# The mLSTM heads of a decoder layer: from the planner's order to a written-out order on all engines

## The chip, the cores and the metric

The kernel runs on one core of a Trainium2 chip. The metric is the device time in microseconds (us). A core has five engines that work side by side: TensorE (PE) multiplies matrices into PSUM banks, VectorE (DVE) and ScalarE (ACT) do elementwise work, GpSimd (POOL) does elementwise work on SBUF, and SyncE (SP) issues most of the loads. Each engine takes its instructions in the order in which they stand in its own program, and waits on semaphores for the results of the others. ACT also issues loads, from its own queue.

## The reference, cut to what matters

One layer: a mixer with four mLSTM heads of 256 columns and a convolution group of 1024 channels beside them, then a gated feed-forward part, for 512 positions of 1024 columns in float32.

```python
mod = cond @ ada_w[l] + ada_b[l]
sh1, sc1, g1, sh2, sc2, g2 = jnp.split(mod[:, None, :], N_MOD, axis=-1)
u = rms_norm(x, mix_pre_g[l]) * (1.0 + sc1) + sh1
proj = u @ w_in[l]
qk_raw, v, o_pre, gates, glu = jnp.split(proj, [...], axis=-1)
qk = jax.nn.silu(causal_dwconv(qk_raw, qk_conv_w[l], qk_conv_b[l]))      # 4 taps
h = mlstm_chunkwise(heads(q), heads(k), heads(v), gates[..., :H] + ..., gates[..., H:] + ...)
h = rms_norm(h, ml_norm_g[l].reshape(H, Dh)).reshape(Bsz, S, D_ML)
h = (h * jax.nn.sigmoid(o_pre))
a, gt = jnp.split(glu, 2, axis=-1)
y = causal_dwconv(a * jax.nn.sigmoid(gt), cv_dw_w[l], cv_dw_b[l])        # 31 taps
y = jax.nn.silu(layer_norm(y, cv_ln_g[l], cv_ln_b[l]))
mix = jnp.concatenate([h, y], axis=-1) @ w_out[l]
x = x + g1 * rms_norm(mix, mix_post_g[l])
...
```

## The kernel before

Every product is made of three matmuls over numbers split into a high and a low part (`mm3`, L198): a weight tile of 512 columns is loaded raw, ACT copies it to the high part and POOL subtracts to get the low one (`w_split`, L176). The pool of split tiles holds 20 (`WSLOTS`), that is ten high-low pairs; raw loads have two buffers (`RAWS`).

The stages, in order: the input's norm and the first six blocks of the GLU projection (written in order), the rest of the GLU projection, the values of head 0 with the gates (`make_v(0)`, L443), the projections of head 0, then a loop over heads that attends with head h while it projects head h+1, then head 3's attention beside the first half of the output projection (`mix_first`, L694), the second half (`mixb`), and the feed-forward part.

The instructions of PE and SP keep the order of the text. Those of DVE, ACT and POOL are placed by a planner, which simulates the program and takes what is ready, by priority; `in_order()` (L74) is a context that ties the DVE, ACT and POOL instructions traced inside it to the order of the text, each engine for itself. Before the change only the opening and a later stretch are so tied.

What a head consists of:

* `head_load(h)` (L485) loads three raw matrices and splits them into twelve pieces of 512 columns.
* `head_proj(h, i)` (L491), i = 0 to 5, is one item: 24 matmuls of 512 columns. Items 0 and 1 are q, 2 and 3 are k: ACT scales (L475), DVE adds three taps (`conv4`, L477), ACT applies Silu (L478). Items 4 and 5 are the output gate: one Tanh on ACT (L503), result `so`.
* `make_E(h)` (L592): PE spreads the running maximum over the partitions (`Mb`), DVE adds the mask (`Md`, L596), ACT takes seven exponentials (L601, L603).
* `make_v(h)`: four value tiles of 24 matmuls of 256 columns, each copied out by ACT (L467).
* `attention(h)` (L508), a generator that gives way between its steps: four score blocks `s` (L516) with a DVE product each (`E`, L517); four output tiles `o` (L527) that ACT reads (L530 to L532); a factor per position (L537 to L540, `fac`), with which DVE scales `hn` four times (L543); then twice: four transposes `hT` (L549), DVE's `so` (L551), ACT's high part `hh` (L554), DVE's low part `hl` (L555).

The scores, outputs, `Mb` and `hT` share two PSUM banks (`atbank`), the projections share four (`mmbank`), the convolution and its norm two (`cvbank`).

Beside this runs the 31-tap convolution: for each of eight channel blocks DVE does 25 taps (L722, 200 in all), ACT and POOL the other five (L716, L718, `SIDE`), then a running mean and square (L732 to L737). All of it is traced once, in front of the head loop, with a low priority (`LATER`), so the planner fills DVE's free time with it. `norm_mean`, `norm_sums` and `norm_rows` (L740 to L763) close the norm. The modulation sums `ada_block(i)` (L159) load 512 KB on ACT's queue and reduce them on DVE (L167); numbers 16 to 23 are traced behind the head loop, with the low priority too, tied behind the last tap; numbers 24 to 39 are tied behind the last `hl`, and `gains` (L843 to L845), which PE turns as `gT` (L646), follow from them.

## Time and profile before

| what | us |
|---|---|
| median of 3 runs | 800.78 (800.26 to 801.73) |
| the profiled execution | 798.5 |
| its span, first to last instruction | 796.7 |
| PE busy | 779.3 |
| DVE / ACT / POOL busy | 475.6 / 380.6 / 438.8 |
| mean granted TensorE clock | 0.995 |

A line of a group gives the line of the kernel, engine, operation, what it writes and reads, the count, then the busy time and the mean of one in ns, then the engine's idle time in front of it and who ended it. A line of the waits gives who waited for whom: total, times, longest. A line of the timeline gives start, duration, engine and instruction; in brackets stands the idle time before it and who ended it. A line of the windows gives the stretch, its length, and the busy time of PE, PEld, DVE, ACT and POOL with the number of instructions, the granted TensorE clock, the busy share of the DMA engines and GB/s.

### The profile page before, as it was taken

What the parts mean: (1) busy time and instruction counts of PE and PEld (TensorE: products, weight loads), DVE (VectorE), ACT (ScalarE), POOL (GpSimd) and SP (SyncE); (2) the same over time, 40 slices, a digit from 0 to 9 for tenths busy, and PEclk for the clock granted to TensorE, in tenths of its full rate; (3) what the DMA queues carried; (4) which work ended last, traced back from release to release, by engine and by line L of the source; (5) the groups of instructions that cost most, each with busy time, mean ns of one, the idle gap of its engine ahead of it and who ended that gap; (6) DMA issues with size and microseconds to landing.
All of it is one profiled execution on the core that took longest, in us unless ns stands there. A gap on an engine that the chain in (4) does not pass through costs nothing.

```text
span 796.7 us, 10339 instructions
## 1 busy us (share of the span) xinstructions
PE 779.3 (98%) x3778; PEld 651.8 (82%) x3778; DVE 475.6 (60%) x732; ACT 380.6 (48%) x710; POOL 438.8 (55%) x359
## 2 busy tenths in 40 slices
PE   8999999999899799999999999999999999999996
PEld 6788898788788688888879988888888888888885
DVE  6779999999997434546868784454444453000014
ACT  6684548757463555571344454444444444122112
POOL 4799759959669433342751475444444444454420
PEclk9999999999999899999999999999999999999999
DMA  8964223222026331426854652222222222222205
GB/s 331 347 237 133 80 73 140 80 94 91 28 107 209 108 133 54 159 105 211 345 186 150 211 195 105 81 82 103 105 107 106 79 107 107 107 105 100 86 0 185
DMA packets 24886, 106.96 MB, mean 134 GB/s; under 512 B 2914, under 2 KB 2946, under 8 KB 17412
## 3 DMA queue, kind: packets, MB, share of 16 engines
q1 hardware_dynamic: 16164, 82.17, 28.8%
q10 hardware_dynamic: 8672, 24.13, 8.7%
q8 instruction: 30, 0.49, 0.3%
q14 instruction: 20, 0.16, 0.1%
HBM read 102.08 MB, written 4.21 MB: 133 GB/s over the span
## 4 chain that ended last, share of the span: by engine, by line
PE 72%; DVE 14%; DMA 5%; issue 3%; POOL 2%; ACT 2%; SPq 0%; DVEq 0%; ACTq 0%; POOLq 0%
PE up L201 10%; PE up L200 10%; PE up L202 10%; DVE cv L722 7%; PE dn L200 5%; PE dn L202 5%; PE dn L201 5%; PE glu L202 2%; PE glu L200 2%; PE glu L201 2%; PE qko L200 2%; PE qko L202 2%; PE qko L201 2%; DMA wglu<-in_w_glu 2%; DMA spare<-in_adaT 2%
## 5 line engine op out<-in xcount | busy, mean ns | idle before, releaser
L722 DVE SCALAR_TENSOR_TENSOR cv<-gt,cvw,cv 128x502 f32<-128x502 f32 (+23 forms) x200 | 134.1, 727 | 1.6 <-ACT cv L710 1.3
L1062 DVE TENSOR_TENSOR fo<-dn,g2r 128x512 f32<-128x512 f32 x8 | 5.5, 685 | 103.1 <-ACT dn_0junk L1058 103.1
L718 POOL TENSOR_TENSOR cs<-cs,cs 128x510 f32<-128x510 f32 (+3 forms) x32 | 43.7, 1368 | 4.4 <-ACT cs L716 4.3
L183 POOL TENSOR_TENSOR wup_1024l<-wup,wup_1024h 128x512 fp32r<-128x512 f32 x20 | 26.9, 1345 | 30.7 <-ACT wup_1024h L182 30.6
L183 POOL TENSOR_TENSOR wup_1536l<-wup,wup_1536h 128x512 fp32r<-128x512 f32 x20 | 27.1, 1354 | 29.6 <-ACT wup_1536h L182 29.5
L183 POOL TENSOR_TENSOR wup_512l<-wup,wup_512h 128x512 fp32r<-128x512 f32 x20 | 26.8, 1340 | 23.6 <-ACT wup_512h L182 21.8
L183 POOL TENSOR_TENSOR wup_0l<-wup,wup_0h 128x512 fp32r<-128x512 f32 x20 | 27.6, 1378 | 20.8 <-ACT wup_0h L182 20.7
L167 DVE SCALAR_TENSOR_TENSOR junk<-ada,cb 128x1024 bf16<-128x1024 f32 x20 | 31.6, 1580 | 8.6 <-DMA ada<-in_adaT 8.4
L201 PE MATMUL up<-u2l,wup_0h 128*128 128x512 f32 (+1 forms) x100 | 36.5, 365 | 0.2 <-DVE u2l L891 0.2
L200 PE MATMUL up<-u2h,wup_0h 128*128 128x512 f32 (+1 forms) x100 | 36.5, 365 | 0.0
L200 PE MATMUL up<-u2h,wup_1024h 128*128 128x512 f32 (+1 forms) x100 | 36.4, 364 | 0.0
L202 PE MATMUL up<-u2h,wup_1536l 128*128 128x512 f32 (+1 forms) x100 | 36.4, 364 | 0.0
L202 PE MATMUL up<-u2h,wup_0l 128*128 128x512 f32 (+1 forms) x100 | 36.4, 364 | 0.0
L200 PE MATMUL up<-u2h,wup_512h 128*128 128x512 f32 (+1 forms) x100 | 36.4, 364 | 0.0
L201 PE MATMUL up<-u2l,wup_512h 128*128 128x512 f32 (+1 forms) x100 | 36.4, 364 | 0.0
L202 PE MATMUL up<-u2h,wup_512l 128*128 128x512 f32 (+1 forms) x100 | 36.4, 364 | 0.0
L200 PE MATMUL up<-u2h,wup_1536h 128*128 128x512 f32 (+1 forms) x100 | 36.4, 364 | 0.0
L201 PE MATMUL up<-u2l,wup_1536h 128*128 128x512 f32 (+1 forms) x100 | 36.4, 364 | 0.0
L202 PE MATMUL up<-u2h,wup_1024l 128*128 128x512 f32 (+1 forms) x100 | 36.4, 364 | 0.0
L201 PE MATMUL up<-u2l,wup_1024h 128*128 128x512 f32 (+1 forms) x100 | 36.3, 363 | 0.0
L183 POOL TENSOR_TENSOR wd_1024l<-wd,wd_1024h 128x512 fp32r<-128x512 f32 x11 | 14.3, 1296 | 29.7 <-ACT wd_1024h L182 29.7
L183 POOL TENSOR_TENSOR wd_0l<-wd,wd_0h 128x512 fp32r<-128x512 f32 x11 | 14.3, 1299 | 27.3 <-ACT wd_0h L182 27.3
(729 smaller groups left out, 2620.3 us busy)
## 6 DMA issues: line engine op xcount, KB each, us to landing
wup<-in_w_up SPq DMA_DIRECT2D x22, 1024.0 KB, 4.8
wqko<-in_w_qko SPq DMA_DIRECT2D x12, 1024.0 KB, 4.8
wd<-in_w_down SPq DMA_DIRECT2D x11, 1024.0 KB, 4.8
ada<-in_adaT ACTq DMA_DIRECT2D x20, 512.0 KB, 5.9
ada<-in_adaT SPq DMA_DIRECT2D x16, 512.0 KB, 7.2
wo<-in_w_out SPq DMA_DIRECT2D x8, 1024.0 KB, 4.8
spare<-in_adaT ACTq DMA_DIRECT2D x12, 512.0 KB, 8.4
wglu<-in_w_glu SPq DMA_DIRECT2D x5, 1024.0 KB, 7.5
```

The costliest lines, as they stand in the source:

```text
L167: t = V.scalar_tensor_tensor(out=junk, in0=r, scalar=1.0, in1=cb, op0=ALU.mult, op1=ALU.mult, accum_out=mod[:, i : i + 1])
L183: (eng or G).tensor_tensor(out=lo[:, :n], in0=src, in1=hi[:, :n].bitcast(F32), op=ALU.subtract)
L200: PE.matmul(ps, a[0], b[0], start=start, stop=False)
L201: PE.matmul(ps, a[0], b[1], start=False, stop=False)
L202: PE.matmul(ps, a[1], b[0], start=False, stop=stop)
L718: G.tensor_tensor(out=side[:, d:], in0=side[:, d:], in1=t[:, d:], op=ALU.add)
L722: last_tap = V.scalar_tensor_tensor(out=cp[:, d:], in0=cvx[j][:, : T - d], scalar=w(CK - 1 - d), in1=cp[:, d:], op0=ALU.mult, op1=ALU.add)
L1062: V.tensor_tensor(out=res[hf], in0=ps, in1=g2r[hf], op=ALU.mult)
```

## The change

Everything from head 0's first projection to the last turn of head 3 stands in one `in_order()` region, so the order of the text is the order on DVE, ACT and POOL too. The weights of all heads, of the values 1 to 3 and of the first half of the output projection are one list of pieces (`spans`); `stream_to(n)` splits them up to piece n and starts the load of the next raw matrix, and each item is followed by it, `LOOK` pieces ahead. The taps and the modulation sums 16 to 23 become a generator, `filler()`: `fill(n)` writes n taps. 92 (`AHEAD`) are traced in front of the region with the low priority, the rest beside the items, as numbers in the code say. A sum comes each eight taps from tap 128 (`ADAB`). `make_v` now gives way after each tile, `attention` once more before the factor and once before `hn`; two small products of the factor move from POOL to DVE. The Silu of q and k comes after the item's taps. The norm's mean goes through the filler; its rows are spread over the output blocks, and head 3's steps come one block earlier.

```diff
+LOOK = 6
+AHEAD = 92
+ADAB = 128
+TAPS = ((4, 4, 1, 2, 5, 6),)
...
-        for q in range(0, KT, 4):
+        for q in range(0, 0 if h else KT, 4):
             r = raws.tile([P, 2048], F32, tag="raw", name=f"wv{h}_{q}")
-            nc.sync.dma_start(r[:, : 4 * n], w_v[h - 1, q // 4] if h else w_v0[q // 4])
-            if h:
-                for i in range(2):
-                    hi, lo = w_split(r[:, i * 2 * n : (i + 1) * 2 * n], f"wv{h}_{q + i}")
-                    wv += [(hi[:, :n], lo[:, :n]), (hi[:, n:], lo[:, n:])]
-            else:
-                wv += [tuple(w[:, :n] for w in w_split(r[:, i * n : (i + 1) * n], f"wv{h}_{q + i}")) for i in range(4)]
+            nc.sync.dma_start(r[:, : 4 * n], w_v0[q // 4])
+            wv += [tuple(w[:, :n] for w in w_split(r[:, i * n : (i + 1) * n], f"wv{h}_{q + i}")) for i in range(4)]
+        if h:
+            stream_to(first_of["v", h] + 4)
+            for hi, lo in vw[h]:
+                wv += [(hi[:, :n], lo[:, :n]), (hi[:, n:], lo[:, n:])]
...
-            if tt > 1:
-                yield
+            if h:
+                stream_to(first_of["v", h] + 4 + 2 * tt)
+            yield
...
-        S.activation(t, t, AF.Silu)
...
-    def head_load(h):
-        pieces = []
+
...
+    def stream_to(n):
+
+        while streamed[0] < min(n, len(spans)):
+            i = streamed[0]
+            load_to(i + 1)
+            first = max(j for j in loaded if j <= i)
+            if i == first:
+                load_to(next((j + 1 for j in range(i + 1, len(spans)) if spans[j][0] is not None), 0))
+            _, name, a, n_, dest = spans[i]
+            dest.append(w_split(loaded[first][:, a : a + n_], f"{name}_{a}"))
+            streamed[0] += 1
...
+    def item(h, i, taps, also=lambda: None):
+
+        stream_to(first_of[h] + 2 * i + 2)
+        head_proj(h, i)
+        fill((taps + 1) // 2)
+        also()
+        n = first_of[h] + 2 * i + 2
+        stream_to(n + LOOK - 1)
+        fill(taps // 2)
+        stream_to(n + LOOK)
+        if i < 4:
+            t = heads[h][1 + i // 2][-1]
+            S.activation(t, t, AF.Silu)
...
+        yield
...
-        G.tensor_tensor(out=dm, in0=dm, in1=dm, op=ALU.mult)
-        G.tensor_tensor(out=ssq, in0=ssq, in1=dm, op=ALU.add)
+        V.tensor_tensor(out=dm, in0=dm, in1=dm, op=ALU.mult)
+        V.tensor_tensor(out=ssq, in0=ssq, in1=dm, op=ALU.add)
         G.tensor_tensor(out=fac, in0=ssq, in1=mhalf, op=ALU.pow)
+        yield
...
+    def conv_taps():
+
+        cv_first(0)
+        for j in range(KT):
+            w = lambda tap: cvw[:, tap * KT + j : tap * KT + j + 1]
+            side = None
+            cp = cps_[j]
+            for d in range(SIDE + 1, CK):
+                last_tap[0] = V.scalar_tensor_tensor(out=cp[:, d:], in0=cvx[j][:, : T - d], scalar=w(CK - 1 - d), in1=cp[:, d:], op0=ALU.mult, op1=ALU.add)
+                s = d - SIDE
+                if s % 4 == 1 and s // 4 < SIDE:
+                    e = s // 4 + 1
+                    t = cvs.tile([P, T], F32, tag="cvs", name=f"cs{j}_{e}")
+                    if e == 1:
+                        V.memset(t[:, :e], 0.0)
+                    S.activation(t[:, e:], cvx[j][:, : T - e], AF.Copy, scale=w(CK - 1 - e))
+                    if side is not None:
+                        G.tensor_tensor(out=side[:, e:], in0=side[:, e:], in1=t[:, e:], op=ALU.add)
+                    else:
+                        side = t
+                if d == CK - 4 and j + 1 < KT:
+                    cv_first(j + 1)
+                yield
...
+    def ada_load(i):
+        adat[i] = adas.tile([P, D], F32, tag="ada", name=f"ada_{i}")
+        nc.scalar.dma_start(adat[i], adaT[i // 2][:, (i % 2) * D : (i % 2 + 1) * D])
+
+    def ada_sum(i):
+        junk = small.tile([P, D], BF16, tag="junk", bufs=1, name=f"junk_{i}")
+        V.scalar_tensor_tensor(out=junk, in0=adat[i], scalar=1.0, in1=cb, op0=ALU.mult, op1=ALU.mult, accum_out=mod[:, i : i + 1])
...
+    def filler():
+        sums = None
+        ada_load(16)
+        ada_load(17)
+        for n, _ in enumerate(conv_taps()):
+            if later and n % 25 == 6:
+                sums = running(*later.pop())
+            if sums is not None:
+                next(sums, None)
+            i, turn = divmod(n - ADAB, 8)
+            if 0 <= i < 8:
+                if turn == 0:
+                    ada_sum(16 + i)
+                elif turn == 3 and i < 6:
+                    ada_load(18 + i)
+            yield
...
+    tc.cur_priority += LATER
+    fill(AHEAD)
+    tc.cur_priority -= LATER
...
+    region = in_order()
+    region.__enter__()
+    stream_to(6)
+    gates_lf()
+    for i in range(3):
+        item(0, i, TAPS[0][i])
+    gates_sum()
+    fill(2)
+    item(0, 3, TAPS[0][3])
+    gates_max()
+    item(0, 4, TAPS[0][4])
+    gates_tok()
+    item(0, 5, TAPS[0][5])
+    make_E(0)
     for h in range(H - 1):
-        head_load(h + 1)
         steps = attention(h)
         if h == 0:
-            head_proj(1, 0)
+            item(1, 0, 3)
         next(steps)
-        head_proj(h + 1, 1 if h == 0 else 0)
+        fill(2)
+        item(h + 1, 1 if h == 0 else 0, 3)
         next(steps)
+        fill(1)
         if h:
-            head_proj(h + 1, 1)
-        head_proj(h + 1, 2)
+            item(h + 1, 1, 3)
+        item(h + 1, 2, 5)
         next(steps)
-        head_proj(h + 1, 3)
+        item(h + 1, 3, 5)
         next(steps)
-        head_proj(h + 1, 4)
+        item(h + 1, 4, 7)
         next(steps)
-        head_proj(h + 1, 5)
+        item(h + 1, 5, 4, lambda: next(steps))
         make_E(h + 1)
-        if h == H - 2:
-            norm_mean()
+        next(steps)
         values = make_v(h + 1)
+        fill(2)
+        next(values)
+        fill(3)
+        next(values)
+        fill(1)
         next(values)
         for _ in steps:
             pass
-        next(values)
-        if h == H - 2:
-            norm_sums()
-
-    tc.cur_priority += LATER
-    for i in range(16, 24):
-        ada_block(i, last_tap)
-    ada_done(16, 24)
-    tc.cur_priority -= LATER
-    gain(0, 16, "mix_post_g")
-    wo = {}
+        fill(2)
+        for _ in values:
+            pass
+        fill(2)
+    while not normed:
+        fill(1)
+    norm_sums()
     steps = attention(H - 1)
+    rows = norm_rows()
     next(steps)
     mix_first(0)
+    fill(2)
     next(steps)
-    norm_rows()
+    fill(1)
     mix_first(1)
+    next(rows)
+    next(rows)
     mix_first(2)
+    next(rows)
+    next(rows)
+    ada_done(16, 24)
+    gain(0, 16, "mix_post_g")
     mix_first(3)
+    next(rows)
+    next(steps)
     mix_first(4)
+    next(rows)
+    next(rows)
     next(steps)
     mix_first(5)
+    for _ in rows:
+        pass
     next(steps)
     mix_first(6)
     next(steps)
-    for n in range(7, 10):
-        mix_first(n)
+    mix_first(7)
+    next(steps)
+    mix_first(8)
+    mix_first(9)
     for _ in steps:
         pass
+    region.__exit__(None, None, None)
+    stream_to(len(spans))
...
```

Of the parts left out, the steps of the gates become functions without a change in them, and `norm_rows` gives way after each row, with the low part of a row written one row later.

More of the change, by code (lines that the diff above doesn't have):

```diff
@@ L639, in decoder_layer, with gates_tok @@
+    def gates_tok():
+        mps = atbank("mtok")
+        mv = mps[:, : NT * H].rearrange("p (t h) -> p t h", t=NT)
+        for tt in range(NT):
+            PE.matmul(mv[:, tt, :], Mr[0][:, tt * P : (tt + 1) * P], ident[:H, :H], start=True, stop=True)
+        V.tensor_tensor(out=em, in0=Fc, in1=mv, op=ALU.add)
+        S.activation(em, em, AF.Exp, scale=-1.0)
+        V.tensor_scalar(out=em, in0=em, scalar1=EPS**0.5, scalar2=None, op0=ALU.mult)
     RD = float(D) ** 0.5
@@ new lines, in decoder_layer, with running @@
+    later = []
+    def running(j, y):
+        mean_of = ys[0] if j == 1 else ysum
+        dl = cvtile(f"ydl{j}")
+        V.scalar_tensor_tensor(out=dl, in0=mean_of, scalar=-1.0 / j, in1=y, op0=ALU.mult, op1=ALU.add)
+        yield
+        yield
+        dst = ysq if j == 1 else dl
+        S.activation(dst, dl, AF.Square, scale=(j / (j + 1.0)) ** 0.5)
+        yield
+        if j > 1:
+            G.tensor_tensor(out=ysq, in0=ysq, in1=dl, op=ALU.add)
+        G.tensor_tensor(out=ysum, in0=mean_of, in1=y, op=ALU.add)
@@ new lines, in decoder_layer @@
+    adat = {}
+    def ada_load(i):
[19 more added lines that the diff above has]
+                    ada_load(18 + i)
+            yield
+        for _ in range(3):
+            yield
+        for _ in running(*later.pop()):
+            yield
+        for _ in range(7):
+            yield
+        for _ in norm_mean():
+            yield
+        normed.append(1)
+        done.append(1)
+        while True:
+            yield
```

175 lines of the change are left out of this document (95 added, 80 removed).

## The prediction

> **What bounds the kernel now.** The page's busy line comes first, then TensorE's (PE) own waits.
>
> ```profile
> PE 779.3 (98%) x3778; PEld 651.8 (82%) x3778; DVE 475.6 (60%) x732; ACT 380.6 (48%) x710; POOL 438.8 (55%) x359
> ```
> ```profile
> PE hT L549 <- ACT E L603: 3.4, 2, 2.5
> ...
> PE hT L549 <- DVE hn L543: 1.7, 2, 0.9
> PE s L516 <- DVE so L551: 1.4, 1, 1.4
> ...
> PE gT L646 <- DVE gains L844: 0.4, 1, 0.4
> ```
>
> The matmuls set the end. The change adds and removes none that matters, so it is worth only what PE now loses by waiting in the heads. The waits are 3.4 + 1.7 + 1.4 = 6.5 us, all at one place: the hand-over from one head to the next, where the transposes hT wait for `hn` and for a PSUM bank, and the scores `s` for a bank that `so` frees. Next the windows by stage: first head's attention, second, third, and a piece of the second.
>
> ```profile
> 158.00:209.20 51.20, 48.97 (x262) 41.40 (x260) 51.20 (x80) 32.20 (x69) 37.93 (x32) 1.00 0.20 72
> 209.20:270.40 61.20, 56.96 (x285) 48.04 (x286) 50.48 (x74) 33.00 (x69) 43.73 (x30) 0.94 0.42 138
> 270.40:326.40 56.00, 56.00 (x298) 47.41 (x297) 22.11 (x36) 27.83 (x60) 22.38 (x20) 1.00 0.21 76
> ...
> 262.40:269.20 6.80, 4.29 (x20) 4.00 (x20) 3.06 (x7) 5.35 (x14) 0.90 (x1) 0.50 0.29 114
> ```
>
> After the length stand PE, weight load, DVE, ACT, POOL, then the granted clock. DVE is busy 51.20 of 51.20 us in the first stretch, with PE idle for 2.23. The third, with the taps done and DVE at 22 us, has no PE idle at all. And the second stall costs twice: the clock falls to 0.50 for 6.8 us. The timeline shows who was late.
>
> ```profile
> 202.11 6.49 DVE L722 SCALAR_TENSOR_TENSOR cv<-gt,cvw,cv 128x495 f32<-128x495 f32 x10
> 202.85 0.60 PE L549 MATMUL hT<-ident,hn 128*128 128x128 f32 x4
> 204.34 0.66 PE L549 MATMUL hT<-ident,hn 128*128 128x128 f32 x4 [0.89 <-ACT E L603]
> 208.51 0.67 DVE L551 SCALAR_TENSOR_TENSOR so<-so,hT 128x512 f32<-128x512 f32 x1
> 209.24 1.13 PE L516 MATMUL s<-q_0c,k_2c 128*128 128x512 f32 x2 [1.37 <-DVE so L551]
> ...
> 211.06 0.81 PE L516 MATMUL s<-q_0c,k_2c 128*128 128x384 f32 x2
> ...
> 259.60 0.28 PE L202 MATMUL v<-wv_5h,ul 128*128 128x256 f32 x1
> 260.69 0.30 PE L549 MATMUL hT<-ident,hn 128*128 128x128 f32 x1 [0.81 <-DVE hn L543]
> 261.87 1.00 PE L549 MATMUL hT<-ident,hn 128*128 128x128 f32 x3 [0.88 <-DVE hn L543]
> 262.54 0.68 DVE L596 TENSOR_TENSOR Md<-Mb,cmask 128x512 f32<-128x512 f32 x1
> 265.38 1.12 PE L549 MATMUL hT<-ident,hn 128*128 128x128 f32 x4 [2.51 <-ACT E L603]
> 266.14 0.56 PE L200 MATMUL v<-wv_0h,uh 128*128 128x256 f32 x1
> ```
>
> hT is ready after 202.85, but ten taps run on DVE until 208.6, and `so` behind them frees the bank late. In the second hand-over `hn` is late, and `Md` with the exps behind it (262.54 to 265.38) later still: DVE did the eight modulation sums in a bunch just before.
>
> **What can be won.** First hand-over: 0.89 + 1.37 = 2.26 us. Second: the second window is 61.20 against 56.00, and the third holds two matmul groups that the second lacks:
>
> ```profile
> 312.43 0.86 PE ytot L743 x2
> ...
> 325.67 0.79 PE ry_s L208 x8
> ```
>
> So an undisturbed head is 56.00 - 1.65 = 54.35 and the second loses 6.85; by hand, 0.81 + 0.88 + 2.51 idle plus half of the 4.29 busy us at half clock (2.15) is 6.35. Together 8.6 to 9.1; I take 9.0.
>
> **The change part by part.** *Taps dealt out.* 92 taps stay ahead of the region, 24 lie in head 0's projections, then 40 in each turn of the head loop (3+2+3+1+5+5+7+4 beside the items, 2+3+1+2+2 beside the values); the last four and the norm's mean fall in the third turn. Two turns are the heavy ones. Their DVE work, from these groups (head stage):
>
> ```profile
> L722 DVE SCALAR_TENSOR_TENSOR cv<-gt,cvw,cv 128x487 f32<-128x487 f32 (+24 forms) x122 | 82.6, 725 | 0.0
> L167 DVE SCALAR_TENSOR_TENSOR junk<-ada,cb 128x1024 bf16<-128x1024 f32 x8 | 13.0, 1630 | 3.9 <-DMA ada<-in_adaT 3.9
> L477 DVE SCALAR_TENSOR_TENSOR k_2c<-qko,vec,k_2c 128x511 f32<-128x511 f32 (+2 forms) x12 | 8.9, 743 | 3.2 <-ACT k_2c L475 3.1
> ...
> L543 DVE TENSOR_SCALAR hn<-hn,fac 128x256 f32<-128x256 f32 x12 | 8.6, 773 | 2.1 <-POOL fac L540 2.1
> L517 DVE SCALAR_TENSOR_TENSOR E<-s,E 128x512 f32<-128x512 f32 (+3 forms) x14 | 7.0, 503 | 10.9 <-PE s L516 10.9
> L732 DVE SCALAR_TENSOR_TENSOR ydl<-ysum,gt 128x512 f32<-128x512 f32 x6 | 6.7, 1109 | 2.7 <-POOL gt L726 2.7
> ```
>
> 40 taps at 6.49/10 = 0.649 are 26.0; four sums (one each 8 taps from tap 128) at 1.63 are 6.5; 12 q/k taps at the same pace 7.8; four `hn` 3.1; four `E` 2.0; 1.6 running means 1.8; Md, two `so` and two `hl` (about 0.7 each) 3.5. Sum 50.7 us; the small operations on 4 or 8 columns add perhaps 1 (estimate: as one running mean). With taps at their record, 0.725, and q/k taps at 0.743, it is 50.7 + 3.0 + 1.1 + 1 = 55.8. The one end lies under PE's 54.35, the other 1.5 over. I take the pace, since `x10` in 6.49 shows instructions overlapping: 51.7, DVE 95% full, but in an order that no longer puts ten taps ahead of `so`.
>
> *What is due when, in the new order.* One projection item and one value tile on PE:
>
> ```profile
> 224.63 0.39 PE L200 MATMUL qko<-uh,wqko_0h 128*128 128x512 f32 x1
> ...
> 230.07 1.47 PE L527 MATMUL o<-v,E 128*128 128x258 f32 x6
> ```
> ```profile
> 199.97 0.28 PE L200 MATMUL v<-wv_0h,uh 128*128 128x256 f32 x1
> ```
>
> An item is 5.44, a value tile 202.85 - 199.97 = 2.88. From the end of item 5, DVE has two taps to finish (1.3), Md (0.7) and four `hn` (3.1): 5.1 us, while PE has three tiles, 8.6: 3.5 us of cover. The exps end 265.38 - 262.54 = 2.84 after Md starts, at about 4.1: cover 4.5. So the hT waits vanish, and with them the low clock. Before `so` DVE still has six taps (3.9) and up to one sum (1.6): it arrives at 5.1 + 3.9 to 5.5 = 9.0 to 10.6 against hT at 8.6 + 0.4. PE has the fourth tile (2.88) before `s` wants that bank. But the written order is so, hl, so, hl, and with ACT's copy before each hl the second bank is free about 2.8 us after the first `so` starts (worked out at the region's end, below). The second `s` wants it 0.4 + 2.88 + 1.8 (211.06 - 209.24) = 5.1 after the first hT. Lag allowed 2.3, lag forecast 0 to 1.6: no wait, or by the record durations some 2. I put 1.0 us for both heavy turns together; ends 0 and 4.
>
> *Head 0's projections.* Gate steps, q/k taps and 24 taps stand on DVE in a fixed order; there is no PE wait now, and `s` follows two items of cover (11 us) after the last k. 0, ends 0 and 1.
>
> *Weights in one stream.* Same splits on ACT and POOL, six pieces ahead (three items, 16 us); SP issues the same loads in the same order, each one matrix ahead, the w_out ones too. ACT 33.0 and POOL 43.7 of 61.2 leave room. Cost 0; without the cover one load's landing, 4.8 us, would be shown once a head. *Two small operations from POOL to DVE*: 0, in the small ones above. *Loads of the sums on ACT's queue*: each waits for a DVE sum three taps earlier; behind it on ACT stand splits with 16 us of lead: 0.
>
> ```profile
> wqko<-in_w_qko SPq DMA_DIRECT2D x12, 1024.0 KB, 4.8
> ```
> ```profile
> 326.40:364.40 38.00, 38.00 (x174) 30.91 (x174) 15.57 (x27) 21.57 (x45) 17.96 (x17) 1.00 0.38 139
> ```
>
> *The last head.* Its attention steps come one output block earlier and the norm's rows are spread over six blocks. DVE has 15.57 and ACT 21.57 of 38.0 there and PE waits for nothing: 0, ends 0 and 0.5; uncovered, a late row's two DVE and two ACT operations would stand in the way, some 0.7 each.
>
> *The end of the region.*
>
> ```profile
> 364.01 1.28 DVE L551 SCALAR_TENSOR_TENSOR so<-so,hT 128x512 f32<-128x512 f32 x2 [5.06 <-PE hT L549]
> 365.49 1.41 DVE L555 SCALAR_TENSOR_TENSOR hl<-so,ghalf,hh 128x512 fp32r<-128x512 f32 x2 [0.20 <-ACT hh L554]
> 366.82 1.22 DVE L167 SCALAR_TENSOR_TENSOR junk<-spare,cb 128x1024 bf16<-128x1024 f32 x1
> ```
>
> Sixteen sums hang behind the last `hl` (366.82), and PE's gT already waits 0.4 for the gains made of them (first waits above). Now so, so, hl, hl take 366.82 - 364.01 = 2.8. Written as so, hl, so, hl, each pair is 0.64 + 0.84 (from the first `so`'s end to its `hl`'s start, ACT's copy) + 0.70 = 2.2, both 4.4: the sums start 1.5 later against PE. I take 1.5 in full; ends 0 (loads, not sums, pace the chain) and 2.5 (a load more is exposed, as far as the DMA wait that the group of sums shows, 3.9 over 8, allows for two of them).
>
> **Sum.** -9.0 + 1.0 + 1.5 = -6.5 us. The profiled execution has 798.5 us (span 796.7 and 1.8 around it): 792.0. The median of the runs, 800.78, lies 2.3 above it: 794.3. With all costs at nothing: 791.8; with 4 + 1 + 0.5 + 2.5 paid: 799.8.
>
> **Rivals.** *DVE becomes the bound.* At 55.8 a turn it is 1.5 over PE, and every wait of the fixed order (a q/k tap waits for its item and ACT's copy, everything else stands behind) adds to it; before, other taps filled such waits. If 3 us of waits come on top, two turns lose 2 x 4.5 = 9, and with 1.5 at gT the 9.0 are gone: 802.3; it turns slower once a turn loses more than 3.75 us. For it: 95% load. Against: four waits a turn come after PE items in which DVE catches up. The Trainium skill (TensorE: Matmul & The Clock Gate, Architectural detail) has ACT and DVE as strict FIFOs, which speaks for it; the ten taps ahead of `so` above agree. *The clock still falls.* If a late `so` keeps PE from ordinary matmuls, each of two hand-overs costs about 2 us of idle and 2.15 of half clock: 794.3 + 6.3 = 800.6 less the 1.0 in it, 799.6. Against: from 202.85 to 209.24 PE idled 2.26 in two parts at a clock of 1.00. By the same page (Part 1; Part 4) an idle window of some 3.4 us halves the clock and transposes do not count as busy; the trace agrees, 259.60 to 266.14 without another matmul and 0.50 from 262.4. *The gain is given back at gT*: if the sums' chain hung on loads and not on `hl`, PE would come 7 us early and wait: 800.8. Against: its first sum follows `hl` at once. *It doesn't do what it says*, the order binding only inside the region while its 92 early taps slide into it: 800 to 801.
>
> **Chances.** Forecast 0.70 (own range 791.0 to 797.5); DVE bound 0.13; clock falls 0.08; given back or no effect 0.09. A measurement tells 0.2%, 1.6 us, from no change. Faster: 0.70, half of the clock case, a third of the last: 0.77. Slower 0.13, the same 0.10. The range 790.5 to 800.5 takes in the forecast's bounds and most of the no-change cases and leaves out the slower one and a little.
>
> **What would show it.** Right: no hT wait on PE, head windows near 54.4 us, clock 1.00 throughout them, `so` within 1.6 us of hT, gT waiting about 2 us, DVE just under full in the first two turns. Wrong: PE waits at `s` or `o` for DVE's `so` or ACT's `hn`, q/k items late for their weights, or a gT wait of many us.

## The result and the profile after

The changed kernel takes 800.07 us (median of 12 runs, 798.43 to 805.71) against 800.36 (12 runs) for the kernel before. The ratio is 1.0003, 95% interval 0.9986 to 1.0020: no difference. The forecast was 794.3. The profiled execution took 798.43 us, its span is 796.6.

The busy line of the page after, then TensorE's waits inside the heads and at gT (us in all, times, longest), each from the changed kernel:

```profile
PE 778.7 (98%) x3778; PEld 651.0 (82%) x3778; DVE 483.2 (61%) x740; ACT 380.6 (48%) x710; POOL 435.6 (55%) x351
```
```profile
PE s L576 <- DVE so L613: 3.9, 4, 2.4
...
PE hT L611 <- DVE hn L605: 1.9, 2, 0.9
PE gT L711 <- ACT wup_512h L187: 1.7, 1, 1.7
```

Before, 6.5 us stood at the hand-overs (hT 3.4 + 1.7, s 1.4) and 0.4 at gT. Now 5.8 stand there and 1.7 at gT. The wait for the exponentials is gone; s waits for `so` instead. The windows by stage (start to first s of the next head, last to the first hT of head 3):

```profile
158.50:208.20 49.70, 49.15 (x263) 41.50 (x261) 44.55 (x71) 31.84 (x70) 29.07 (x22) 1.00 0.27 96
208.20:268.50 60.30, 55.22 (x286) 46.03 (x286) 56.89 (x82) 34.45 (x73) 44.20 (x32) 1.00 0.37 119
268.50:325.00 56.50, 56.34 (x296) 47.48 (x297) 31.98 (x50) 28.71 (x62) 25.79 (x20) 1.00 0.19 69
325.00:363.00 38.00, 38.00 (x173) 30.84 (x173) 19.48 (x32) 23.10 (x49) 17.48 (x14) 1.00 0.40 139
```

The granted clock is 1.00 in the second window (0.94 before), so that part of the loss is gone. But the second window is still 60.30 long (61.20 before): PE is idle for 5.1 of it, and DVE, the third figure behind the length, is at 56.89 where 51.7 was forecast. From the starts of the matmuls in the two traces, stage by stage (first matmul to first matmul, us):

```
stage                          before   after   change   forecast
start to s of head 0           157.88   158.51   +0.63     0
s of head 0 to s of head 1      51.36    49.65   -1.71  }
s of head 1 to s of head 2      61.21    60.32   -0.89  }  -8.0
s of head 2 to s of head 3      55.87    56.33   +0.46  }
s of head 3 to its hT           37.06    37.09   +0.03     0
its hT to gT for gains          39.67    41.03   +1.36    +1.5
gT to the last matmul's end    387.47   387.49   +0.02     0
```

The heads give 2.1 us, gT takes 1.4 and the first row 0.6; the runs below, e4 aside, show 157.1 to 160.1 in it, most of them with the same code ahead of the heads, so it is taken for scatter. Of the 8 us, 6 didn't come, nearly all of them at the second hand-over. There the DVE timeline of the changed kernel reads (start, duration, instruction, how many):

```profile
256.58 0.68 DVE L662 TENSOR_TENSOR Md<-Mb,cmask 128x512 f32<-128x512 f32 x1
257.18 5.23 DVE L605 TENSOR_SCALAR hn<-hn,fac 128x256 f32<-128x256 f32 x4
262.33 1.50 DVE L783 SCALAR_TENSOR_TENSOR cv<-gt,cvw,cv 128x495 f32<-128x495 f32 x2
263.74 1.15 DVE L462 COPY v<-ones 128x8 f32<-128x8 f32 x1
264.80 3.03 DVE L783 SCALAR_TENSOR_TENSOR cv<-gt,cvw,cv 128x493 f32<-128x493 f32 x4
267.74 0.68 DVE L613 SCALAR_TENSOR_TENSOR so<-so,hT 128x512 f32<-128x512 f32 x1
```

DVE isn't idle for a moment. Four `hn` take 5.23 us, a copy of eight columns 1.15, and `so` starts 8.0 us after the first hT (259.77). One turn earlier the copy took 0.17, `so` started 3.7 us after the first hT, and the four `hn` read:

```profile
200.98 2.19 DVE L605 TENSOR_SCALAR hn<-hn,fac 128x256 f32<-128x256 f32 x4
```

POOL in the stretch of the second turn:

```profile
255.31 1.85 POOL L188 TENSOR_TENSOR wqko_0l<-wqko,wqko_0h 128x512 fp32r<-128x512 f32 x1
257.12 1.29 POOL L818 TENSOR_TENSOR ysq<-ysq,ydl 128x512 f32<-128x512 f32 x1
258.37 1.35 POOL L819 TENSOR_TENSOR ysum<-ysum,gt 128x512 f32<-128x512 f32 x1
259.67 1.32 POOL L188 TENSOR_TENSOR wqko_512l<-wqko,wqko_512h 128x512 fp32r<-128x512 f32 x1
260.95 2.66 POOL L792 TENSOR_TENSOR cs<-cs,cs 128x508 f32<-128x508 f32 x2
```

Six POOL instructions stand back to back from 255.31 on, most 1.3 us long, and each `hn` is about as long as one of them. All sixteen `hn` of the changed kernel as a group (shortest, median, longest in ns):

```profile
L605 DVE TENSOR_SCALAR hn<-hn,fac x16: 340/1374/1397, 201.0 to 360.0; 128x256 f32<-128x256 f32 x16
```

So one and the same instruction takes either 0.34 us or 1.37, and the long ones fall beside POOL work. The Trainium skill (SBUF — State Buffer, Who interferes with whom) states that VectorE and GpSimd share a pair of ports as a lock held for a whole instruction, that copies and tensor_scalar in the two-port modes and instructions with two SBUF inputs contend for it, and that an instruction with at most one SBUF input outside these modes does not. The trace agrees: the taps, which read one operand from SBUF and one from PSUM, take 704 to 750 ns, all 200 of them, though most lie beside POOL work.

The second suspect is the pace of the taps. Before, ten of them took 6.49 us, 0.649 each. In the changed kernel, in a stretch that holds nothing else:

```profile
192.18 5.34 DVE L783 SCALAR_TENSOR_TENSOR cv<-gt,cvw,cv 128x494 f32<-128x494 f32 x7
```

That is 0.763 each. A single tap is as long as before. But the planner let two channel blocks alternate, and the written-out order takes one block after the other, so every tap adds into the bank into which the tap before it has just written.

### The profile page after: what moved, and what is told of

Its sections match the earlier page's. It is cut to its first block, busy times and chain, and to the rows that moved or that the text cites. A ratio compares the mean times of both kernels' runs of the same rounds, so it can differ in the third digit from the quotient of the medians.

```text
span 796.6 us, 10322 instructions
## 1 busy us (share of the span) xinstructions
PE 778.7 (98%) x3778; PEld 651.0 (82%) x3778; DVE 483.2 (61%) x740; ACT 380.6 (48%) x710; POOL 435.6 (55%) x351
## 4 chain that ended last, share of the span: by engine, by line
PE 78%; DVE 13%; DMA 3%; ACT 3%; issue 2%; POOL 1%; ACTq 0%; DVEq 0%; POOLq 0%
PE up L206 10%; PE up L207 10%; PE up L205 10%; DVE cv L783 6%; PE dn L206 5%; PE dn L207 5%; PE dn L205 5%; PE qko L205 4%; PE qko L207 3%; PE qko L206 3%; PE glu L206 2%; PE glu L205 2%; PE glu L207 2%; DMA spare<-in_adaT 2%; PE glu L352 2%
## 5 line engine op out<-in xcount | busy, mean ns | idle before, releaser
L783 DVE SCALAR_TENSOR_TENSOR cv<-gt,cvw,cv 128x506 f32<-128x506 f32 (+24 forms) x200 | 139.9, 732 | 3.3 <-ACT cv L773 0.8
L790 ACT ACTIVATE cs<-gt,cvw 128x511 f32<-128x511 f32 (+4 forms) x40 | 28.1, 714 | 4.7 <-POOL cs L792 2.9
```

Of the source, the lines that this page charges most:

```text
L783: last_tap[0] = V.scalar_tensor_tensor(out=cp[:, d:], in0=cvx[j][:, : T - d], scalar=w(CK - 1 - d), in1=cp[:, d:], op0=ALU.mult, op1=ALU.add)
L790: S.activation(t[:, e:], cvx[j][:, : T - e], AF.Copy, scale=w(CK - 1 - e))
```

## The experiments

Two theories at first. **Price**: the order is good, but DVE's instructions cost more in it than forecast, by taps in series and by POOL. **Order**: `so` stands behind `hl` and taps, or the sums stand behind the last `hl`. Later a third question arose, whether VectorE's order was the cause of the losses before. All ratios are to runs of the kernel before on the same chip.

```
run             median  ratio, 95% interval       s head 0   hT head 3   gT to
                us                                to hT 3    to gT       first up
before          800.36                            205.50     39.67       23.69
after           800.07  1.0003 (0.9986, 1.0020)   203.40     41.03       23.71
e1_pairs        797.49  0.9967 (0.9954, 0.9979)   201.39     40.75       23.71
e2_so_first     799.38  0.9984 (0.9974, 0.9995)   202.70     41.28       25.33
e3_hn_act       796.95  0.9966 (0.9952, 0.9980)   198.64     42.55       25.34
e4_float        811.51  1.0141 (1.0123, 1.0159)   201.32     42.17       23.68
e5_three        794.52  0.9929 (0.9906, 0.9951)   199.14     41.65       25.30
e6_early_sums   803.32  1.0038 (1.0025, 1.0051)   203.32     39.63       29.82
e7_all          792.21  0.9893 (0.9877, 0.9910)   199.16     39.12       23.71
e8_quiet_pool   793.28  0.9909 (0.9891, 0.9927)   197.74     40.89       23.69
e9_hold_adds    795.22  0.9938 (0.9916, 0.9960)   199.40     41.44       25.33
e10_hold_all    794.54  0.9927 (0.9911, 0.9942)   198.60     39.46       27.29
e11_before_quiet 788.75 0.9855 (0.9841, 0.9869)   195.75     39.12       23.71
e12_before_side1 796.43 0.9958 (0.9943, 0.9973)   202.19     39.12       23.71
e13_quiet_all   792.66  0.9912 (0.9896, 0.9927)   196.50     39.41       27.32
```

The last three columns are from the starts of the matmuls in each profiled execution: the heads, the end of the region, and the way from gT to the first matmul of the up projection. The 1.6 us that e2, e3, e5 and e9 lose in the last column were not followed up. The profiled executions of e5 and e9 took 3 us more than the medians.

### e1: the taps of two channel blocks alternate

```
-        for j in range(KT):
+        def block(j):
...
+        run = [[0, block(0), 0], [1, block(1), 6]]
+        turn = 0
+        while any(r[1] for r in run):
+            r = run[turn % 2]
+            turn += 1
...
+            if next(r[1], "end") == "end":
+                r[0] += 2
+                r[1] = block(r[0]) if r[0] < KT else None
...
+            yield
```

> After, with one edit: the filler takes the taps of two channel blocks in turn, so that no tap stands directly behind the tap that it adds to. Theory A (taps in one chain cost 0.765 us a tap against 0.64 where two blocks alternate, which fills DVE in the second turn): start-to-start of taps inside the region falls to about 0.64, DVE busy in the second turn by 4 to 5 us, the waits hT and s of the second hand-over from 5.4 us to under 1.5; the run 3.5 to 5 us faster than the kernel before. Theory B (hn and the copy of ones are slow because POOL works beside them, 5.2 us for four hn against 2.2 a turn earlier): taps may quicken, but hn stays late, gain under 2 us. Theory C (any fixed order stalls DVE behind its waits): DVE idle grows as its work shrinks, no gain.

Seven taps at the same place of the e1 timeline:

```profile
192.11 4.51 DVE L783 SCALAR_TENSOR_TENSOR cv<-gt,cvw,cv 128x491 f32<-128x491 f32 x7
```

0.644 each, and the kernel is 2.6 us faster than the changed kernel. So 0.763 was the price of taps in series. The second head's stretch, first s to first s, falls from 60.32 to 56.43; 1.9 of these 3.9 us come back in the first and the third. The four `hn` of the second turn still took 5.28 us.

### e2: both so ahead of both hl

```
             S.activation(hi, t, AF.Copy, scale=g)
-            last_lo[0] = V.scalar_tensor_tensor(out=lo, in0=t, scalar=g, in1=hi.bitcast(F32), ...)
-            hy[2 * h + e] = (hi, lo)
+            turned.append((e, t, g, hi, lo))
+        for e, t, g, hi, lo in turned:
+            last_lo[0] = V.scalar_tensor_tensor(out=lo, in0=t, scalar=g, in1=hi.bitcast(F32), ...)
+            hy[2 * h + e] = (hi, lo)
```

> After, with one edit: at each hand-over DVE does so, so, hl, hl in place of so, hl, so, hl. Theory A (the written order costs one ACT copy at each hand-over and at the start of the sums): the sums 24 to 39 start 1.5 us earlier behind hT, the wait at gT falls from 1.7 to about 0.3, the wait of the second s block (1.0 and 0.3 us at 210.9 and 270.6) goes: 2 to 2.5 us faster than after. Rival (the sums' chain is paced by its loads): gT waits as before, under 1 us gained.

TensorE's waits in e2:

```profile
PE s L576 <- DVE so L614: 2.9, 2, 2.4
PE hT L612 <- DVE hn L605: 2.2, 3, 0.9
PE gT L714 <- ACT wup_512h L187: 2.0, 1, 2.0
```

The first `so`, which costs 2.4, is late for a reason ahead of it; the order of so and hl is worth 0.7 us in the heads. That gT's wait would fall was wrong: the sums' chain is set by more than the place of `hl`.

### e3: hn on ScalarE

```
-    V.tensor_scalar(out=hv, in0=hv, scalar1=fac[:, tt : tt + 1], ...)
+    S.activation(hv, hv, AF.Copy, scale=fac[:, tt : tt + 1])
...
-        make_E(h + 1)
         next(steps)
+        make_E(h + 1)
```

> After, with one edit: the four products hn are done by ACT, ahead of the exps, not by DVE. Theory B (hn and what it meets from POOL are what is late at the hand-over): the wait hT <- hn of 1.9 us goes and DVE reaches so 3 to 5 us earlier in the second turn: 4 to 5 us faster than after. Theory A: the same DVE time is saved in the second turn only (hn 5.2 us there), so also 3 to 4 us there, but taps stay at 0.765 apart; in the first turn DVE gains 2.2 us and its 0.7 + 1.0 us of waits at s shrink by half. If ACT is the late one instead, hT waits for ACT and nothing is gained.

TensorE's waits in e3:

```profile
PE gT L711 <- DVE gains L1024: 3.2, 1, 3.2
PE s L576 <- DVE so L613: 1.5, 2, 0.8
```

The heads shrink by 4.8 us, the most of any single edit that leaves the computation whole. A part goes at gT (+1.5 against the changed kernel) and 1.6 on the way to the up projection, so that the time falls by 3.1 only, less than the 4 to 5 expected.

### e4: the taps given back to the planner, the heads still in order

```
-AHEAD = 92
+AHEAD = 200
```

All 200 taps and the sums 16 to 23 are traced ahead of the heads with a low priority, so the planner places them.

> After, but all 200 taps and the sums 16 to 23 are traced ahead of the region with the low priority, for the planner to place, as in the kernel before; the heads keep their written order. Theory A: taps go back to 0.64 apart as the planner alternates two blocks, and DVE is full again until about 230 us as before; the hand-over waits depend on what the planner puts ahead of hn and so: between the before kernel's 9 us of loss and 2. Theory C (the written order of the heads is what costs): as slow as after or slower, with taps at 0.64.

TensorE's longest wait in e4:

```profile
PE aT L686 <- DVE ga L680: 10.8, 1, 10.8
```

Slower. At the hand-overs TensorE waited 0.8 us in all, but in head 0's gates DVE had planner-placed taps ahead of `ga`, and TensorE waited 10.8 us in one piece; another 3.3 went inside the first head's attention. A written-out order holds its own instructions together, but not against what the planner puts between them.

### e5, e6 and e7: the edits together, and the sums earlier

e5 is e1 + e2 + e3. e6 is the changed kernel with sums 24 to 28 moved between the last head's output products and their loads issued ahead. e7 is all of it.

```
     norm_sums()
+    spare.append(upool.tile([P, KT, T], F32, tag="ul", name="spare"))
+    for i in range(24, 30):
+        later_load(i)
...
+    later_sum(24)
     mix_first(5)
...
-    for i in range(24, 40):
+    for i in range(29, 40):
         ada_block(i, last_lo[0])
```

> The three edits that each gave about 1 to 3 us are put together: the taps of two channel blocks alternate, the four hn of a head run on ScalarE ahead of the exps, and the two so come ahead of the two hl. Theory (VectorE was the bound in the heavy turn by its taps in series and by hn beside GpSimd; what the hand-overs give back is then lost at the transpose of the gains, whose sums start after the last hl): the third head's first s of the second hand-over (s#4) starts at or before 262.5 us, waits on so and hn are under 1.5 us in all at the two hand-overs, the first hT of the last head starts at 354 to 356.5 us (363.37 before), but the gT transpose waits 2.5 to 5 us for the gains; the time is 794 to 796.5, so about the better of the single edits and not the sum of their gains (3.4 + 2.6 + 0.7 = 6.7 us, 793.4). Rival (the gains are independent): 793.4 or less and gT's wait as in the changed kernel, 1.7.

> Only the place of the modulation sums 24 to 39 is changed against the changed kernel: six loads are issued as soon as the last head's projections are done, five of the sums (24 to 28) run on VectorE between the output products of the last head, and eleven stay behind the last hl. Theory (the transpose of the gains is held by this chain and not by TensorE): the wait of gT falls from 1.7 us to under 0.5, worth 1.2 to 1.9 us: 798.2 to 799. Rival (the chain is paced by the loads or the end is set elsewhere, so an earlier start gives nothing): 800 and the wait still 1.5 or more. Possible cost: the early sums delay the last head's so or E products on VectorE; then a wait of s or hT in the last head of over 1 us shows it.

> The three edits of the run before last together with the early sums. Theory (gains at the hand-overs were given back at gT): gT's wait is under 0.7 us, so that the whole of the earlier first hT (354 to 356.5 us against 363.37 before) reaches the end: gT's transposes follow the first hT by about 39.2 us as in the kernel before (403.04 less 363.37 less 0.5), and the time is 790.5 to 793.5. Rival (something else after the last head, the weights' stream or the rows of gains, sets the end): 795 or more, with another wait of 2 us or more between the last head and the up projection.

e5's time is as expected, with 2.4 us of wait at gT; its starts are some 2 us later than expected, of which 1.2 stood there before the first head. e6 alone became slower, although gT came when it should (39.63). ScalarE's timeline of e6 shows why:

```profile
384.10 0.63 ACT L191 ACTIVATE wo_0h<-wo 128x512 fp32r<-128x512 f32 x1 [14.83 <-DMA x<-in_x]
```

The planner put loads on ACT's queue ahead of weight splits; the splits stood 14.83 us behind them, and from gT to the up projection it was 29.82, 6.1 more than in the changed kernel. TensorE waits there 2.6 for the last split of `wo` and 1.2 for `u2l`, and the mean clock of this stretch is 0.94. In e7, where `hn` is also on ACT, the planner chose otherwise, and the whole gain arrived. Its waits in the heads are all there is:

```profile
PE s L580 <- ACT E L676: 1.2, 1, 1.2
PE o L591 <- ACT hn L595: 1.0, 1, 1.0
PE hT L616 <- ACT E L676: 0.3, 1, 0.3
```

e7 is faster than both kernels by 1.1% (0.9893, 0.9877 to 0.9910).

### e8: the changed kernel with less on GpSimd

It leaves out the side taps' and the running sums' additions, 44 of GpSimd's 351 instructions, so these parts are missing from the output.

```
-    if side is not None:
-        G.tensor_tensor(out=side[:, e:], in0=side[:, e:], in1=t[:, e:], op=ALU.add)
-    else:
+    if side is None:
         side = t
...
-    if j > 1:
-        G.tensor_tensor(out=ysq, in0=ysq, in1=dl, op=ALU.add)
-    G.tensor_tensor(out=ysum, in0=mean_of, in1=y, op=ALU.add)
+    if j == 1:
+        G.tensor_tensor(out=ysum, in0=mean_of, in1=y, op=ALU.add)
```

> The changed kernel without GpSimd's additions of the convolution's side taps and of the running sums over the channel blocks (the output lacks these parts); VectorE's and ScalarE's instructions stay as they are, and GpSimd keeps the low parts of the weights. Theory (an hn of VectorE stands still while a GpSimd instruction runs, 0.34 us each alone and 1.38 beside one): the four hn of the second turn, 5.23 us in the changed kernel, take 1.4 to 3.5 us, the copy of the ones 0.16 instead of 1.15 if GpSimd is idle beside it, the waits of s and hT at the second hand-over fall by 1.5 to 3.5 us, and the time is 796.5 to 799. Rival (hn is slow there by itself, or by ScalarE): hn stays at 5 us and the time at 800.

DVE's timeline of e8 at the second hand-over, then TensorE's wait for `so` in all heads:

```profile
255.33 2.19 DVE L605 TENSOR_SCALAR hn<-hn,fac 128x256 f32<-128x256 f32 x4
257.43 1.50 DVE L783 SCALAR_TENSOR_TENSOR cv<-gt,cvw,cv 128x495 f32<-128x495 f32 x2
258.85 0.17 DVE L462 COPY v<-ones 128x8 f32<-128x8 f32 x1
258.97 3.04 DVE L783 SCALAR_TENSOR_TENSOR cv<-gt,cvw,cv 128x493 f32<-128x493 f32 x4
261.93 0.68 DVE L613 SCALAR_TENSOR_TENSOR so<-so,hT 128x512 f32<-128x512 f32 x1
```
```profile
PE s L576 <- DVE so L613: 1.2, 3, 0.7
```

DVE has the same instructions in the same order. `hn` 5.23 has become 2.19, the copy 1.15 has become 0.17, the taps are as long as before, and 793.28 is below the range expected. GpSimd's additions cost the changed kernel some 7 us (800.07 less 793.28, on two chips).

### e9 and e10: the additions held back, nothing left out

```
+    def let_go(still=False):
+        for out, a, b in held:
+            t = G.tensor_tensor(out=out, in0=a, in1=b, op=ALU.add)
+            if not still:
+                tc.add_manual_dep(t.ins, last_hn[0].ins.name, ...)
...
+    holding[0] = True
     item(h + 1, 4, 7)
...
+    let_go()
     values = make_v(h + 1)
```

> The changed kernel with GpSimd's additions of the fill (side taps and running sums) that fall between the fifth item of a turn and hn held back until the last hn of that turn is done; nothing is left out. Theory (hn loses its time to a GpSimd instruction that runs beside it): in the second turn the four hn take 1.4 to 3.5 us instead of 5.23, the waits of s and hT at the second hand-over (together about 5 us) fall by 1.5 to 4 us, and the time is 796 to 798.5, above the 793.28 of the run without the additions, because the held additions then stand beside the copy of the ones and hl, and GpSimd's weight parts come later. Rival (it was the smaller amount of GpSimd work as such that helped, not its place): 799 to 801, with hn short and the waits where they were.

> Alternating taps, the held additions, the two so ahead of the two hl, and the early sums 24 to 28, with hn on VectorE. Theory: the second hand-over loses under 1.5 us and gT waits under 0.5; the first hT of the last head starts at 354 to 357 us, the time is 790.5 to 793.5, the same as with hn on ScalarE (792.21) to within 1.5. Rival (VectorE has too much again with hn, and the early sums reorder the loads of the up weights as they did alone): 795 or more.

GpSimd and VectorE in e9:

```profile
258.26 1.29 POOL L188 TENSOR_TENSOR wqko_512l<-wqko,wqko_512h 128x512 fp32r<-128x512 f32 x1
260.63 1.28 POOL L777 TENSOR_TENSOR cs<-cs,cs 128x509 f32<-128x509 f32 x1 [1.08 <-DVE hn L605]
```
```profile
258.31 2.18 DVE L605 TENSOR_SCALAR hn<-hn,fac 128x256 f32<-128x256 f32 x4
261.82 0.17 DVE L462 COPY v<-ones 128x8 f32<-128x8 f32 x1
```

With the same amount of work on GpSimd, only later, `hn` takes 2.18 and the copy 0.17; the wait for `hn` is gone and the heads are 4.0 us shorter than in the changed kernel. So for `hn` it is where the GpSimd work stands that counts, and 795.22 is below the range expected. e10 adds the alternating taps, the order of so and the early sums; its heads and gT gain 6.4 us against the changed kernel, of which 3.6 are lost on the way to the up projection (27.29), as in e6. The time, 794.54, is between the two expectations.

### e11: the control, the kernel before without the same additions

The edit is that of e8, in the kernel before, and the same parts are missing from the output.

> The kernel before, without the same additions of GpSimd as in the run of the changed kernel that left them out (the output lacks these parts). It is the control of that run. Theory (in the kernel before the planner fills VectorE's queue around the hand-overs with other things, and its losses are ten taps ahead of so, and the sums in a bunch ahead of hn): it gains less than the changed kernel did (6.8 us): 796 to 800. Rival (GpSimd's additions cost every order of the heads the same, and the change itself brings nothing): 792.5 to 795.

The rival was more than right: 788.75, 11.5 us below the 800.27 of the kernel before on that chip. TensorE's windows of e11, from first s to first s, then to the hT of head 3:

```profile
158.35:207.07 48.72, 48.72 (x263) 41.59 (x262) 48.55 (x82) 33.20 (x73) 20.65 (x18) 1.00 0.22 76
207.07:261.19 54.12, 54.12 (x288) 46.08 (x287) 45.33 (x74) 32.14 (x69) 26.95 (x21) 1.00 0.46 156
261.19:317.04 55.85, 55.85 (x298) 47.27 (x296) 22.91 (x37) 27.73 (x60) 23.30 (x21) 1.00 0.21 76
317.04:354.10 37.06, 37.06 (x167) 29.96 (x166) 15.19 (x27) 21.02 (x44) 17.71 (x16) 1.00 0.40 142
```

PE is busy in every microsecond of the heads, with an order of the planner's and with DVE at 48.55 of 48.72 in the first window. What the prediction held against VectorE's order is still there: seven of the eight modulation sums stand ahead of the second turn's `hn` (229.66 to 249.75), and at the first hand-over eight taps, ten before, stand ahead of `so` (205.88):

```profile
200.76 5.21 DVE L720 SCALAR_TENSOR_TENSOR cv<-gt,cvw,cv 128x494 f32<-128x494 f32 x8
```

So the losses of the kernel before need GpSimd's additions; VectorE's order alone does not make them. What was late at its second hand-over begins on GpSimd and reaches `fac` through ScalarE's queue. In the kernel before:

```profile
248.12 1.77 DVE L732 SCALAR_TENSOR_TENSOR ydl<-ysum,gt 128x512 f32<-128x512 f32 x1 [2.66 <-POOL gt L726]
249.92 0.63 ACT L734 ACTIVATE ydl<-ydl 128x512 f32<-128x512 f32 x1 [3.79 <-DVE ydl L732]
249.97 2.21 POOL L737 TENSOR_TENSOR ysum<-ysum,gt 128x512 f32<-128x512 f32 x1 [0.63 <-DVE ydl L732]
251.06 2.57 ACTq L165 DMA_DIRECT2D ada<-in_adaT  x2
251.07 2.19 DVE L167 SCALAR_TENSOR_TENSOR junk<-ada,cb 128x1024 bf16<-128x1024 f32 x1
253.68 0.17 ACT L530 ACTIVATE dm<-o 128x1 f32<-128x1 f32 x1 [2.12 <-DVE junk L167]
...
257.18 1.03 POOL L540 TENSOR_TENSOR fac<-ssq,mhalf 128x4 f32<-128x4 f32 x1
```

and in e11:

```profile
244.76 0.16 ACT L530 ACTIVATE dm<-o 128x1 f32<-128x1 f32 x1
...
248.32 1.03 POOL L540 TENSOR_TENSOR fac<-ssq,mhalf 128x4 f32<-128x4 f32 x1
```

VectorE's running mean `ydl` waited 2.66 us for GpSimd's last addition of a channel block, and ScalarE 3.79 for that mean. Then ScalarE stood behind two loads of modulation sums, which waited for a sum on VectorE that took 2.19 beside GpSimd's running sum (1.2 alone). So it came to the last output of the head, `dm`, 8.9 us later than in e11, and `fac` came 8.9 us later too; 2.2 of these were there from the first hand-over (first s of head 1 at 209.24 and 207.07). The planner's order has a part in this, since it put the mean and the loads ahead of `dm` on ScalarE; it places things a little differently in e11 too. How much of the 11.5 us is the standstill of VectorE and how much GpSimd's full queue was not separated.

### e12: a whole kernel with the side taps on VectorE

```
-SIDE = 5
+SIDE = 1
```

Thirty-two taps go from GpSimd and ScalarE to VectorE; nothing is left out.

> The kernel before with SIDE = 1 instead of 5: of each channel block four taps more run on VectorE (32 in all, at 0.65 us 21 us of VectorE) and GpSimd's 32 additions of side taps (41 us at 1.29) and ScalarE's 32 products fall away; nothing is left out. Theory (the losses at the hand-overs of the kernel before come from GpSimd's backlog and from VectorE and GpSimd standing still for each other): the waits of hT and s, 6.5 us, fall to under 3, and the time is 791 to 797; the bound of 788.75 isn't reached, since the running sums stay on GpSimd. Rival (VectorE, busy throughout the first head's attention, is the bound, and any tap more on it costs): 800 or more, with the first hand-over's loss above its 2.3 us.

The stretch of the second window of the kernel before (209.2 to 270.4), read in e12:

```profile
209.20:270.40 61.20, 59.60 (x308) 50.10 (x307) 61.13 (x90) 30.28 (x65) 37.38 (x29) 1.00 0.27 95
```

VectorE has more work and is busy for 61.13 of 61.20 us, yet PE loses 1.6 where it lost 4.24, and the clock stays at 1.00 (0.94 before). The first two heads take 48.72 and 55.26 us, the first without a wait, although eleven taps stand there between `hn` and `so` (195.87 to 204.53, with `Md` and a running mean among them). The third head then takes 61.15 (55.87 before), since the taps reach into it and TensorE waits 2.0 for DVE's `E`, so 796.43 is all that remains. A full VectorE costs time there; but the first hand-over shows that a full VectorE and taps ahead of `so` need not make TensorE wait.

### e13: what the changed kernel loses beside GpSimd

e8 with the alternating taps, so ahead of hl, and the early sums.

> The changed kernel without GpSimd's additions, as in the run at 793.28, and with the alternating taps, the two so ahead of the two hl, and the early sums 24 to 28. Theory (4.5 us between that run and the kernel before without the same additions, 788.75, are the change's own losses: about 2 us in the heads by taps in series and by so behind hl, and 1.8 at gT by sums that start later): 788.3 to 790, gT's wait under 0.3, waits of s and hT under 0.5. Rival (the remainder lies elsewhere, in the written-out order as such): 791.5 to 793.5.

Its heads take 196.50 (e8: 197.74, e11: 195.75) and gT 39.41 (40.89, 39.12): these three edits remove most of what the change itself had cost. But the time is 792.66, in the rival's range and above the theory's, for 3.6 us are lost again on the way to the up projection (27.32); TensorE waits there 2.8 for `un` and `u2l`. ScalarE in e13:

```profile
384.45 0.60 ACT L743 ACTIVATE mixa0junk<-mixa 128x512 bf16<-128x512 f32 x1 [8.86 <-DVE mg L1054]
```

The weight splits stand on ACT behind this square, which stands behind eleven sums on DVE. How the planner came to that order, and whether it is what delays `un` and `u2l`, was not tried.

## Why the prediction was wrong, step by step

**What can be won (9.0 us): right in size, wrong in cause.** Against e11's undisturbed windows of 48.72 and 54.12 the kernel before loses 51.36 - 48.72 = 2.64 and 61.21 - 54.12 = 7.09, together 9.7. But the prediction put it to VectorE's order, "ten taps run on DVE" ahead of `so` and "DVE did the eight modulation sums in a bunch just before". In e12 eleven taps ahead of `so`, and in e11 the bunch of sums ahead of `hn`, cost TensorE nothing. The losses need GpSimd's additions, which reach PE through instructions that stand still (four `hn` of the first turn took 4.25 us before, 1.13 in e11) and through `fac`. A new order of VectorE doesn't take these away.

**What is due when ("two taps to finish", four `hn` at 3.1, `so` at 9.0 to 10.6, residual 1.0 for both heavy turns): this is the step that failed.** Its times count from the end of item 5, which lies at 195.01 and 251.07 in the two turns. `Md` was to start at 1.3; it started at 5.4 and 5.5. In the second turn four taps, a running mean, a sum and three small operations stand before it, where the step counted two taps. The pace of the taps is a part of that: 0.649 was read from a stretch where two blocks alternate, in the new order it is 0.763, 40 x 0.114 = 4.6 us a turn, and with alternating taps (e1) `Md` starts at 4.1 and 3.7. So the 3.5 us of cover were used up in both turns. Then the price of four `hn`, 3.1, was a mean of two kinds of instruction, 0.34 and 1.37: they took 2.19 and 5.23, and the copy 0.17 and 1.15. `so` started at 12.4 and 16.7. The 4.3 us between the two turns are nearly all GpSimd's, 3.0 in `hn` and 1.0 in the copy; with the additions held back (e9) `so` of the second turn starts at 12.3. Against e11's windows the two turns lose 0.9 + 6.2 = 7.1 us where the step had 1.0. DVE's 56.89 in the second window lies over the high end of its load, 55.8, too.

**The clock: right.** It stays at 1.00, and hT no longer waits for the exponentials, though it still waits 1.9 for `hn`. The price of the rival in which the clock falls was added up wrongly: two hand-overs of 2 and 2.15 us are 8.3 and not 6.3, so by its own terms it gives 801.6; that case did not come.

**Head 0's projections, the weights' stream, the last head (0 each): right.** From the first q item to the first s it is 41.77 before and 41.76 after; no wait of PE for a weight stands in the heads; the last head takes 37.09 for 37.06.

**The end of the region (+1.5): right in size**, 1.36. The reason given, the place of the sums behind so, hl, so, hl, doesn't hold by itself: e2 undid that order and gT still waited 2.0. Sums that stand beside GpSimd take 2.2 us in place of 1.2, which e2 left as it was; whether this, the loads or the small operations on `gains` set the rest was not separated.

**The rivals.** "DVE becomes the bound" had the right mechanism, a fuller DVE in a fixed order, at a chance of 0.13, and its price of 4.5 us a turn was too high for the first turn (0.9) and too low for the second (6.2). "Given back at gT" shows only once the hand-overs are mended: e3 and e5 lose there what e7 keeps.

## What to carry to other kernels

Before a VectorE queue is put in a new order, look at the shortest, median and longest duration of each group on it and not at the mean: here two peaks, 0.34 and 1.37 us, meant that another engine held it up, and a new order of VectorE alone didn't mend that. Price an instruction by the neighbours that it will have in the new order, those on its own engine (does it add to what the one before it wrote?) and those on GpSimd. And test the suspected cause in the kernel before as well: only e11 and e12 showed that VectorE's order alone did not make its losses.

## What the runs showed of the hardware

* VectorE and GpSimd stand still for each other: `hn` (128x256) takes 0.34 or 1.37 us, a copy of eight columns 0.17 or 1.15, a sum over 1024 columns 1.2 or up to 2.3, and on the other side a GpSimd addition of 512 columns 1.29 or 2.2. Taps with one operand in PSUM, 0.70 to 0.75 for all 200, are not affected.
* Taps that add one after the other into the same PSUM bank follow each other at 0.763 us, taps of two banks in turn at 0.644 (e1) and 0.649 (before), at the same duration of one.
